# Issuing the first two loads of an attention-score kernel from two engines instead of one

## The chip, the cores and the metric

The kernel runs on one NeuronCore of a Trainium2 chip. The metric is the device time of one execution in microseconds (us): 201.15 us is the median of three executions of the kernel before the change, which took 201.14, 201.15 and 201.38 us. A profiled execution gives the trace on which all other numbers rest; it spans 199.8 us on its own scale, which begins with the first recorded instruction. All times inside an execution are told as microseconds from that start.

## The reference: scaled scores of queries and keys

The inputs are `q` and `k`, both float32 of shape (8, 8, 512, 64): batch, heads, sequence, head dimension. The output is float32 of shape (8, 8, 512, 512).

```python
def reference(q, k):
    scale = 1.0 / np.sqrt(q.shape[-1])
    return (np.einsum('bhqd,bhkd->bhqk', q, k) * scale).astype(np.float32)
```

There are 64 independent products of a 512 x 64 matrix with a 64 x 512 matrix. The inputs are 16.78 MB together and the output is 67.11 MB, so the kernel writes four times what it reads.

## The kernel before: loads, casts, transposes, scores, stores

The batch is cut into four *units* of two batch entries. A unit `v` has one load of `k` and one of `q`, each of 2 MB. They are called k0, q0, k1, q1, k2, q2, k3, q3 here. SyncE issues every one of them, and every transfer goes through SyncE's one hardware DMA queue in that order.

```python
    def xf(v):
        return bigs[(0, 1, 2, 1)[v]]....          # three big buffers, shared with the stores

    def load(v, x):                               # x = 0: k, x = 1: q
        return nc.sync.dma_start(out=xf(v)[:, x], in_=(k_r, q_r)[x][v]...
                                 ).then_inc(load_sems[2 * v + x], 16)

    tc.no_tile_sem_insts.add(load(0, 0).ins.name)   # k0 goes out in the program's opening,
    tc.close()                                      # ahead of the barrier that ends it
    ...
    for n in range(1, 2 * (UNITS - 1)):             # q0, k1, q1, k2, q2 follow the barrier
        load(n // 2, n % 2)
    for x in range(2):                              # k3, q3 reuse the buffer of unit 1:
        nc.sync.wait_ge(sem["ready"], 3 + x)        # wait for the casts of k1 and q1
        load(UNITS - 1, x)
    for g in range(ALL):                            # sixteen stores of 4 MB, in the same queue
        nc.sync.wait_ge(sem["act"], 4 * g + 4)
        nc.sync.wait_ge(sem["dve"], 4 * g + 4)
        nc.sync.dma_start(out=out_r[g], in_=store_buffer(g)...).then_inc(store_sems[g % 3], 16)
```

GpSimd turns each loaded block into bf16, in the order k0, q0, k1, q1 and so on, two instructions for a block. `ready` counts the finished blocks.

```python
    for v in range(UNITS):
        for x in range(2):
            nc.gpsimd.wait_ge(load_sems[2 * v + x], 16)
            ...
            for s in range(2):
                cast = nc.gpsimd.tensor_copy(out=dst, in_=src)     # 128 x 2048, f32 -> bf16
            cast.then_inc(sem["ready"], 1)
```

TensorE transposes the blocks and then computes the scores. The work on the scores is cut into sixteen groups `g` of 4 MB of output; a group has eight pairs of matmuls. ScalarE and VectorE alternate in taking a pair out of PSUM, with the scale multiplied in, into the group's store buffer. Groups 1 and 2 write into buffers that held loads, so they wait until those loads have been cast; from group 3 on, a group waits for an earlier store to land.

```python
    def scores(g, p):
        ...
            if p == 0 and w == 1:
                if g < 3:
                    pe.wait_ge(sem["ready"], (2, 6, 8)[g])
                else:
                    pe.wait_ge(store_sems[g % 3], g // 3 * 16)
            ins = pe.matmul(out=pss[pair % 3][:, w, :], lhsT=qz[:, n, i + w], rhs=keys[:, n], ...)
```

The stores of the groups are called s0 to s15 here. There are three store buffers.

Of the kernel before, what the change touches and what calls it, by code (L numbers as in the profile page):

```python
# [5 lines left out]
def kernel(  # L6
# [5 lines left out]
    nc = tc.nc  # L12
# [3 lines left out]
    UNITS = B // 2  # L16
# [22 lines left out]
    load_sems = [nc.alloc_semaphore(f"load{n}") for n in range(2 * UNITS)]  # L39
# [3 lines left out]
    q_r = q.rearrange("(v b) g (m j) d -> v (b g m) (j d)", b=2, j=R)  # L43
    k_r = k.rearrange("(v b) g (m j) d -> v (b g m) (j d)", b=2, j=R)
# [25 lines left out]
    def xf(v):  # L70
        return bigs[(0, 1, 2, 1)[v]].rearrange("p x i k -> p (x i k)").rearrange(
            "p (x s c) -> p x s c", x=2, s=2)
# [1 line left out]
    def store_buffer(g):  # L74
        return bigs[(0, 2, 1)[g % 3]]

    def load(v, x):
        return nc.sync.dma_start(out=xf(v)[:, x],
                                 in_=(k_r, q_r)[x][v].rearrange("p (s c) -> p s c", s=2)
                                 ).then_inc(load_sems[2 * v + x], 16)  # L80


    tc.no_tile_sem_insts.add(load(0, 0).ins.name)
    tc.close()
    tc.compile()  # L85


    for n in range(1, 2 * (UNITS - 1)):
        load(n // 2, n % 2)
    for x in range(2):  # L90
        nc.sync.wait_ge(sem["ready"], 3 + x)
        load(UNITS - 1, x)
# [62 lines left out]
    for g in range(ALL):  # L155
        c = g + CHUNKS
# [88 lines left out]
```

## Time and profile before

| Quantity | Before |
|---|---|
| median time | 201.15 us |
| span of the profiled execution | 199.8 us |
| TensorE (matmul) busy | 98.2 us, 49% |
| VectorE busy | 106.1 us, 53% |
| ScalarE busy | 84.7 us, 42% |
| GpSimd busy | 39.5 us, 20% |
| DMA traffic | 83.95 MB, mean 420 GB/s |
| loads of k / q, 2 MB each, median from issue to landing | 15.4 / 17.8 us |
| stores, 4 MB each, median from issue to landing | 21.8 us |

A busy share is the part of the span in which an engine had an instruction in execution. The sixteen DMA engines of the core are shared by everything that moves data. A DMA is *issued* by an engine's instruction queue (SPq is that of SyncE), the time until *landing* is that until its last completion signal has arrived, and it includes time spent behind earlier transfers in the same queue.

The chain of waits starts at the last instruction and goes back, at each step, to whatever released it. The timeline lists instructions in order of time, and merges neighbours of one kind: "x14" after a row says that it holds fourteen of them.

### The profile page before, as it was taken

The numbers are of one execution on the slowest core, as the hardware profiler recorded it, in microseconds if no ns is written. First come the engines' busy times: TensorE is split into PE (matmuls) and PEld (weight loads), VectorE is DVE, ScalarE is ACT, GpSimd is POOL, SyncE is SP. The second block draws the span as 40 slices with busy tenths as digits, with TensorE's granted clock in tenths as the row PEclk, the third lists the DMA queues.
The fourth block names the chain that finished last, engine by engine and source line by source line (L and its number), as shares of the span: only waits on it lengthen the run. The fifth ranks groups of instructions, "written<-read, shape, count | busy, mean of one in ns | idle before, by whom it ended". The sixth has DMA issues, their size and how long they took to land.

```text
span 199.8 us, 1074 instructions
## 1 busy us (share of the span) xinstructions
PE 98.2 (49%) x377; PEld 46.7 (23%) x384; DVE 106.1 (53%) x98; ACT 84.7 (42%) x97; POOL 39.5 (20%) x22
## 2 busy tenths in 40 slices
PE   0027660375695637676547646873737373720000
PEld 0026530141442314243124313330202020200000
DVE  4815691074798928476917682767364545440000
ACT  2004670264686726465626653664444343520000
POOL 1299999986000000000000000000000000000000
PEclk9999996578799978889957995799696969685555
DMA  6999999999999999999999999999999999999996
GB/s 207 433 436 426 430 433 433 430 387 430 426 443 426 426 425 431 439 430 423 426 443 433 426 423 436 436 430 423 430 443 430 423 426 436 433 426 430 436 426 275
DMA packets 5509, 83.95 MB, mean 420 GB/s; under 512 B 384, under 2 KB 384, under 8 KB 384
## 3 DMA queue, kind: packets, MB, share of 16 engines
q1 hardware_dynamic: 5504, 83.89, 98.7%
q8 instruction: 3, 0.05, 0.1%
q14 instruction: 2, 0.02, 0.0%
HBM read 16.78 MB, written 67.11 MB: 420 GB/s over the span
## 4 chain that ended last, share of the span: by engine, by line
DMA 53%; DVE 12%; POOL 12%; PE 9%; issue 1%; ACT 1%; SPq 0%
DMA out_dram<-big 42%; POOL xb L122 12%; DVE big L212 10%; DMA big<-in_q_dram 8%; PE ps L145 7%; DMA big<-in_k_dram 4%; PE tp L130 3%; DVE qz L184 2%; DVE kT L184 1%; ACT big L209 1%; SPq L95 0%
## 5 line engine op out<-in xcount | busy, mean ns | idle before, releaser
L145 PE MATMUL ps<-kT,qz 128*128 128x512 bf16 x249 | 78.4, 447 | 63.0 <-DMA out_dram<-big 31.1
L212 DVE TENSOR_SCALAR big<-ps 128x1024 f32<-128x1024 f32 x64 | 77.0, 1223 | 52.0 <-PE ps L145 49.9
L209 ACT ACTIVATE big<-ps 128x1024 f32<-128x1024 f32 x64 | 64.9, 1024 | 71.1 <-PE ps L145 67.9
L145 PEld LDWEIGHTS ps<-kT,qz 128*128 128x128 bf16 x256 | 24.8, 108 | 109.7 <-DMA out_dram<-big 34.5
L122 POOL CAST xb<-big 128x2048 bf16<-128x2048 f32 x16 | 38.8, 2466 | 7.0 <-DMA big<-in_k_dram 6.0
L130 PE MATMUL tp<-identity,xb 128*128 128x128 f32 x104 | 18.9, 343 | 13.6 <-POOL xb L122 13.6
L130 PEld LDWEIGHTS tp<-identity,xb 128*128 128x128 f32 x104 | 17.2, 184 | 17.6 <-issue 16.5
L184 DVE COPY kT<-tp 64x512 f32<-64x512 f32 x14 | 9.7, 694 | 9.0 <-PE tp L130 8.5
L184 ACT COPY kT<-tp 64x512 f32<-64x512 f32 x14 | 8.1, 577 | 14.1 <-PE tp L130 14.0
L184 DVE COPY qz<-tp 64x512 f32<-64x512 f32 x12 | 8.3, 694 | 4.4 <-PE tp L130 4.1
L189 DVE MEMSET qz<- 128x4096 uint32 x2 | 6.9, 3472 | 3.6 <-PEq L85 2.8
L184 ACT COPY qz<-tp 64x512 f32<-64x512 f32 x12 | 7.5, 622 | 2.0 <-PE tp L130 1.8
L130 PE MATMUL ps<-identity,xb 128*128 128x128 f32 x24 | 5.4, 412 | 1.2 <-POOL xb L122 1.2
L130 PEld LDWEIGHTS ps<-identity,xb 128*128 128x128 f32 x24 | 5.0, 226 | 1.6 <-POOL xb L122 1.6
L184 DVE COPY qz<-ps 64x512 f32<-64x512 f32 x4 | 2.8, 695 | 1.9 <-PE ps L130 1.7
L184 ACT COPY qz<-ps 64x512 f32<-64x512 f32 x4 | 2.5, 626 | 2.2 <-PE ps L130 2.2
L184 ACT ACT_TABLE_LOAD x1 | 1.3, 1283 | 1.9 <-PEq L85 1.9
L184 DVE COPY kT<-ps 64x512 f32<-64x512 f32 x2 | 1.4, 694 | 0.3 <-PE ps L130 0.3
L184 ACT COPY kT<-ps 64x512 f32<-64x512 f32 x2 | 1.2, 578 | 0.5 <-PE ps L130 0.5
L102 POOL MEMSET identity<- 128x128 f32 x1 | 0.2, 205 | 1.5 <-POOLq L85 1.5
L104 POOL TENSOR_SCALAR_AFFINE_SELECT identity<-identity 128x128 f32<-128x128 f32 x1 | 0.3, 294 | 0.2 <-POOL identity L102 0.2
L229 POOL MEMSET const-float32-0.0<- 128x1 f32 x1 | 0.1, 100 | 0.2 <-issue 0.2
(3 smaller groups left out, 0.3 us busy)
## 6 DMA issues: line engine op xcount, KB each, us to landing
out_dram<-big SPq DMA_DIRECT2D x16, 4096.0 KB, 21.8
big<-in_k_dram SPq DMA_DIRECT2D x4, 2048.0 KB, 15.4
big<-in_q_dram SPq DMA_DIRECT2D x4, 2048.0 KB, 17.8
```

The costliest lines, as they stand in the source:

```text
L102: nc.gpsimd.memset(identity, 0.0).then_inc(sem["ident"], 1)
L104: nc.gpsimd.affine_select(out=identity, in_=identity, compare_op=mybir.AluOpType.not_equal, fill=1.0, base=0, pattern=[[-1, P]], channel_m ...
L122: cast = nc.gpsimd.tensor_copy(out=dst, in_=src)
L130: ins = pe.transpose(out=dst[:, w], identity=identity, in_=xw[:, c % SLOTS * W + w])
L145: ins = pe.matmul(out=pss[pair % 3][:, w, :], lhsT=qz[:, n, i + w], rhs=keys[:, n], start=True, stop=True)
L184: copy(out=dst, in_=src[:, h]).then_inc(sem["moved"], 1)
L189: engine.memset(qz[:, v * N:(v + 1) * N], 0.0).then_inc(sem["zeroed"], 1)
L209: lambda o, ps: nc.scalar.mul(out=o, in_=ps, mul=scale),
L212: lambda o, ps: nc.vector.tensor_scalar(out=o, in0=ps, scalar1=scale, scalar2=None, op0=mult),
L229: nc = _bacc.Bacc("TRN2", target_bir_lowering=False, num_devices=1)
```

## The change: k0 from SyncE and q0 from ScalarE

The load of q0 is moved from SyncE, where it followed k0 and the opening barrier, to ScalarE, ahead of that barrier. It is for having both blocks of the first unit on their way at once. The other six loads and all stores stay on SyncE, in their order. Nothing is added to or taken from the number of transfers, their sizes or the computation.

```diff
-    def load(v, x):
-        return nc.sync.dma_start(out=xf(v)[:, x],
-                                 in_=(k_r, q_r)[x][v].rearrange("p (s c) -> p s c", s=2)
-                                 ).then_inc(load_sems[2 * v + x], 16)
-
-
-    tc.no_tile_sem_insts.add(load(0, 0).ins.name)
+    def load(v, x, queue=nc.sync):
+        return queue.dma_start(out=xf(v)[:, x],
+                               in_=(k_r, q_r)[x][v].rearrange("p (s c) -> p s c", s=2)
+                               ).then_inc(load_sems[2 * v + x], 16)
+
+
+
+    for x, queue in enumerate((nc.sync, nc.scalar)):
+        tc.no_tile_sem_insts.add(load(0, x, queue).ins.name)
     tc.close()
     tc.compile()
 
 
-    for n in range(1, 2 * (UNITS - 1)):
+    for n in range(2, 2 * (UNITS - 1)):
         load(n // 2, n % 2)
```

## The prediction, made before the changed kernel was run

> **What bounds the kernel now.** I read the rows by slice first, because a kernel with 84 MB of traffic and no engine above 53% is likely to be bound by its transfers.
>
> ```profile
> DMA  6999999999999999999999999999999999999996
> GB/s 207 433 436 426 430 433 433 430 387 430 426 443 426 426 425 431 439 430 423 426 443 433 426 423 436 436 430 423 430 443 430 423 426 436 433 426 430 436 426 275
> ...
> q1 hardware_dynamic: 5504, 83.89, 98.7%
> ```
>
> Each figure stands for one fortieth of the span, 5.0 us. From the second slice to the last but one the DMA engines are busy throughout, at about 430 GB/s, and one queue holds all of it. 83.89 MB at 430 GB/s are 195.1 us; with 1.8 us before the first packet and some 2 us for the slow first packets and the last landings that is the whole span of 199.8 us. So the transfers are the bound, and a change can move the end in two ways only: by making the stream of transfers start earlier or run faster, or by tearing a hole in it.
>
> Next I read the chain of waits in order of time, for its opening, and then the timeline, for how far each issue lies ahead of the transfer it feeds.
>
> ```profile
> 0.74 7.88 DMA big<-in_k_dram
> 8.62 0.06 issue
> 8.68 4.82 POOL xb L122 x2
> 13.49 0.05 issue
> 13.54 4.85 POOL xb L122 x2
> ```
>
> k0 is issued at 0.74 and lands at 8.62; GpSimd begins its casts 0.06 us later. Each block costs it 4.82 to 4.86 us.
>
> ```profile
> 1.92 0.34 SPq L78 DMA_DIRECT2D big<-in_q_dram  x1
> ...
> 8.68 34.21 POOL L122 CAST xb<-big 128x2048 bf16<-128x2048 f32 x14 [6.03 <-DMA big<-in_k_dram]
> 43.62 4.84 POOL L122 CAST xb<-big 128x2048 bf16<-128x2048 f32 x2 [0.74 <-DMA big<-in_q_dram]
> ```
>
> The second row is the important one: fourteen casts, seven blocks, without a gap from 8.68 to 42.89. GpSimd is as fast as the loads, so anything that delays its first cast delays its next six blocks by as much. Only q3, the eighth, has waited for its load, 0.74 us.
>
> ```profile
> 37.99 2.31 PE L145 MATMUL ps<-kT,qz 128*128 128x512 bf16 x5 [7.83 <-POOL xb L122]
> ...
> 48.52 1.96 PE L145 MATMUL ps<-kT,qz 128*128 128x512 bf16 x5 [2.14 <-POOL xb L122]
> ```
>
> These are the starts of groups 1 and 2. Both waited for GpSimd (7.83 and 2.14 us): the buffer they fill has to be cast first, blocks 6 and 8 of the `ready` waits.
>
> ```profile
> 30.95 0.40 SPq L96 DMA_DIRECT2D out_dram<-big  x1
> ...
> 47.15 0.39 SPq L96 DMA_DIRECT2D out_dram<-big  x1
> ...
> 57.32 0.37 SPq L96 DMA_DIRECT2D out_dram<-big  x1
> ...
> 63.93 0.37 SPq L96 DMA_DIRECT2D out_dram<-big  x1
> ...
> DMA to landing us min/median/max: 16.0/21.8/22.6
> ```
>
> Those are the issues of s0 to s3, from the timeline of SyncE. The last row is of all sixteen stores. A store alone takes 9.72 us of the DMA engines: the chain has s3 landing at 82.96 and s6 at 112.11, so (112.11 - 82.96) / 3. A landing after 21.8 us means that such a store was issued a good 12 us before it was needed. The shortest, 16.0 us, is s2 (57.32 to 73.28); s1 comes next with 16.4. The early stores have the least lead.
>
> How much lead, exactly? The packet records of the trace, in order of their starts, have the first packet of s0 at 42.06, that of s1 at 51.78 and that of s2 at 61.63. The lead of the issue over the first packet is 11.1, **4.63** and **4.31** us. Part of that is needed: k0, issued into an idle queue at 0.74, had its first packet at 1.76, so an issue takes 1.0 us to bite. The delay that the queue can swallow is therefore 10.1 us at s0, 3.6 us at s1 and 3.3 us at s2.
>
> **What the Trainium skill says.** "DMA: Bandwidth & Descriptors", section "Issuing engines are not separate DMA queues", says that transfers started by different engines run on the same 16 DMA engines and interleave, and that only issue time is saved. The kernel before has one queue in use for loads and stores, so its trace neither supports nor denies this. The same page, section "Queues, rings and completion order", says that each DMA engine takes packets in turn from the queues that have work for it. Again no run of before shows two such queues. In its section on latency the page gives about 0.6 us to the first byte of a hardware-issued transfer; here it was 1.0 us from the start of the issue (0.39 us of which is the issue itself). I use the measured number.
>
> **The change part by part.**
>
> *Removed:* one issue on SyncE after the barrier, 0.34 us. k1 is then issued at about 1.9 instead of 2.31. This is worth nothing, as k1's packets did not begin before 12.3.
>
> *Added:* one issue on ScalarE in the opening, about 0.4 us, at about 0.74. ScalarE has no work before its copies at 15.61, and SyncE's own issue fits ahead of the same barrier, so I put this at nothing as well.
>
> *Moved:* q0 reaches the DMA engines about 1.2 us sooner, but they were not idle. Its packets no longer stand behind those of k0, they alternate with them. A load is 128 packets of 16 KB, eight for each DMA engine, of 0.61 us. Both loads together still take until 13.5, when q0 landed before (1.92 + 11.6, its least time to landing). k0 ends at the fifteenth or so of sixteen packets instead of the eighth: 13.5 - 0.6 = 12.9 us instead of 8.62. **k0 lands 4.3 us later, q0 no sooner.** The two blocks are cast one after another on GpSimd, k0 first, so having q0 sooner would have helped nothing: before, q0 landed just as the cast of k0 ended, at 13.49.
>
> *What follows:* the casts run from 12.9 on without a gap. They shift by 4.3 us up to block 7, and q3 by 4.3 - 0.74 = 3.5 us. k3 is issued at 23.32 + 4.3 = 27.6 and q3 at 28.23 + 4.3 = 32.5. Their packets are due about 31.8 and 36.7, so both still come in time, by over 3 us. s0 goes out at 35.2, 10.1 - 4.3 = 5.8 us in hand. s1 goes out at 47.15 + 4.3 = 51.4, its first packet is possible at 52.4, and the queue ran dry at 51.8: a **hole of about 0.7 us** (4.3 - 3.6). s2 goes out at 57.32 + 3.5 = 60.8, bites at 61.8, and is due at 61.63 + 0.7 = 62.3: no further hole. s3 at 67.4 has about 3 us in hand. From group 4 on, the waits are for landed stores, and the lead of about 12 us is restored.
>
> *The sum:* 0 for the issues, +0.7 for the hole, -0.3 for two corrections. First, the sixteen DMA engines do not run dry together: s0 finished over a stretch of 1.2 us, and an engine that lags loses less. Second, the opening is slow before: the 128 packets of k0 took 0.71 us in the mean instead of 0.61, 8 x 0.1 = 0.8 us for each engine, and two queues with requests outstanding could cover some of this. 201.15 + 0.7 - 0.3 is 201.55, told as 201.5.
>
> **The rivals.**
>
> *A, the delay is hidden entirely.* If ScalarE's issue comes half a microsecond after SyncE's, k0 gets a packet's start, lands at 12.3, and the shift of 3.7 lies at the edge of the 3.6 that s1 can swallow. If the DMA engines served SyncE's queue first, k0 would land at 8.6 as before and nothing at all would move. For it: the bulk of the work is bound by transfers, and the stream is the same. Time 201.0 to 201.3.
>
> *B, the opening gets faster.* Two queues fill the slow first packets; up to 0.8 us are to be had there. Against it: the sixteen engines are each busy from their first packet on, only slowly[...]. Without a hole it makes 200.4 to 200.8.
>
> *C, GpSimd becomes the bound of the first 60 us.* If k0 lands last (ScalarE issues first), the shift is 4.9 or more, and a queue that has run dry restarts as slowly as it did at 1.76, with first packets of about 1.4 us instead of 0.61. Then s1 leaves a hole of 1.3 + 0.8 us, and 202.5 to 203.2 is the time. For it: the leads are small and every term of the shift is one way. Against it: it needs several terms at their worst.
>
> **Range and chances.** The main path is 201.3 to 202.0, A and B pull below, C above. A range of 200.6 to 202.4 should hold it eight times in ten. Two per cent would be 4 us. For the slow side that needs a hole of 4 us, so a shift near 8, and no load can hold k0 back that far; for the fast side it needs bandwidth above the 430 GB/s at which the queue runs. Within 2% is nearly sure: 0.96; faster 0.01; slower 0.03.
>
> **What would show each step right or wrong.** The DMA queue part of the page must list two hardware queues, the new one with 2 MB. In the chain or the timeline GpSimd's first cast must start at about 12.9; a start at 8.7 means that the queues are not served in turn, and one at 13.5 or later that q0 went ahead. The casts must run on without a gap to about 51.9. The issues of s1 and s2 must move from 47.15 and 57.32 to about 51.4 and 60.8, and the fall in GB/s must be in the slice from 50 to 55 us. If the slices there stay at 430 while the issue has moved, my lag of 1.0 us is too long. The prediction would be wrong altogether if ScalarE's issue held up the opening barrier, or if two queues changed the packet time of 0.61 us.

## The result and the profile after

The changed kernel takes 202.70 us (median of 6 executions, 202.35 to 202.97) against 201.28 us for the kernel before beside it (6 executions, 201.14 to 201.60). The ratio is 1.0069, 95% interval 1.0055 to 1.0082: 1.4 us slower, within 2%, and beyond the upper end of the predicted range, 202.4.

The rows by slice and the queues of the changed kernel, from its page:

```profile
DMA  6999999999999999999999999999999999999996
GB/s 254 424 430 443 427 421 430 404 362 424 424 440 430 424 427 434 424 424 440 430 417 421 437 440 424 417 427 424 430 434 427 421 421 434 434 427 421 427 424 284
...
q1 hardware_dynamic: 5360, 81.79, 96.3%
q10 hardware_dynamic: 144, 2.10, 2.5%
```

The second queue, q10, is there, with the 2.10 MB of q0; q1 is SyncE's. The first slice moved more than before (254 against 207 GB/s): the opening is indeed fuller. But the slice from 40 to 45 us fell from 387 to 362, and later slices show 417 to 424 again and again, where the kernel before has 423 at the least. The DMA row shows no dip, and the slice from 50 to 55 us, where the prediction put the hole, has 424.

The chain of waits in order of time, and the casts in the timeline of GpSimd:

```profile
0.74 12.49 DMA big<-in_k_dram
13.23 0.05 issue
13.28 19.58 POOL xb L124 x9
...
13.28 38.21 POOL L124 CAST xb<-big 128x2048 bf16<-128x2048 f32 x16 [10.64 <-DMA big<-in_k_dram]
```

k0 lands at 13.23 instead of 8.62, q0 at 13.40 and so hardly sooner than before (13.48), and all sixteen casts follow one another to 51.49. From the timeline of SyncE come the issues of s0, s1 and s2:

```profile
35.78 0.40 SPq L98 DMA_DIRECT2D out_dram<-big  x1
...
50.70 0.39 SPq L98 DMA_DIRECT2D out_dram<-big  x1
...
60.49 0.37 SPq L98 DMA_DIRECT2D out_dram<-big  x1
```

They are 4.8, 3.6 and 3.2 us later than before. The first packet of s1 starts at 51.96, so its lead is 1.3 us where it was 4.6; that of s2 is 1.4, where it was 4.3.

Did the DMA engines run dry? By the packet records they were idle for 0.01 us in the mean between 51 and 53 us, as little as in the kernel before. So the 1.2 us by which the span grew (201.0 against 199.8) are not in a hole. The windows from 64 to 184 us show where they are. The first row is of the kernel before, the second of the changed one; the columns are the stretch, its length, the busy time and number of instructions of TensorE, weight loads, VectorE, ScalarE and GpSimd, then TensorE's clock, the DMA share and GB/s:

```profile
64.00:184.00 120.00, 67.67 (x250) 28.67 (x252) 68.87 (x64) 57.78 (x64) 0.00 (x0) 0.84 1.01 431
...
64.00:184.00 120.00, 70.62 (x260) 29.33 (x260) 71.86 (x67) 59.20 (x66) 0.00 (x0) 0.82 1.01 427
```

The DMA engines are busy all the time in both, but move 1% less in a microsecond, long after the changed opening is over. The packet records say the same: the 16 KB packets of the last thirteen stores take 0.616 us in the mean, and took 0.612 before. From the first packet of s0 to the end of the last packet there are 158.45 us, and there were 157.38: +1.07 us. Of these, 0.85 us are packet time (the sum over all packets of the stores, a sixteenth of it for each engine: 157.59 against 156.74); the rest lies between packets or in how far apart the engines end. Another 0.16 is that s0 itself begins at 42.22 instead of 42.06.

### The profile page after: what moved, and what is told of

It reads as the page before. It is cut to its first block, busy times and chain, and to the rows that moved or that the text cites. A ratio compares the mean times of both kernels' runs of the same rounds, so it can differ in the third digit from the quotient of the medians.

```text
span 201.0 us, 1081 instructions
## 1 busy us (share of the span) xinstructions
PE 98.9 (49%) x384; PEld 45.6 (23%) x384; DVE 106.1 (53%) x98; ACT 85.0 (42%) x97; POOL 38.9 (19%) x22
## 4 chain that ended last, share of the span: by engine, by line
DMA 46%; POOL 18%; DVE 13%; PE 9%; issue 2%; ACT 1%; SPq 0%
DMA out_dram<-big 40%; POOL xb L124 18%; DVE big L214 10%; DMA big<-in_k_dram 6%; PE ps L147 6%; PE tp L132 3%; DVE qz L186 2%; DVE kT L186 1%; ACT big L211 1%; SPq L97 0%
## 5 line engine op out<-in xcount | busy, mean ns | idle before, releaser
L147 PE MATMUL ps<-kT,qz 128*128 128x512 bf16 x256 | 80.4, 449 | 58.8 <-DMA out_dram<-big 28.5
L124 POOL CAST xb<-big 128x2048 bf16<-128x2048 f32 x16 | 38.2, 2500 | 10.6 <-DMA big<-in_k_dram 10.6
L132 PE MATMUL tp<-identity,xb 128*128 128x128 f32 x104 | 19.6, 351 | 18.2 <-POOL xb L124 18.2
L132 PEld LDWEIGHTS tp<-identity,xb 128*128 128x128 f32 x104 | 17.9, 190 | 22.5 <-issue 21.5
L132 PE MATMUL ps<-identity,xb 128*128 128x128 f32 x24 | 3.5, 304 | 1.4 <-POOL xb L124 1.4
L132 PEld LDWEIGHTS ps<-identity,xb 128*128 128x128 f32 x24 | 3.3, 162 | 1.6 <-POOL xb L124 1.6
```

Of the source, the lines that this page charges most:

```text
L132: ins = pe.transpose(out=dst[:, w], identity=identity, in_=xw[:, c % SLOTS * W + w])
```

## The experiments

Two theories stood at the start. **Shift**: what counts is that the casts, and with them the issues of the first stores, come late. **Queue**: what counts is the second queue, or the interleaved opening, which could leave the sixteen DMA engines in an order in which all later packets are slower. All times below are medians, with the kernel before run on the same chip.

### The shift alone, the queue alone

The first experiment keeps one queue and has GpSimd wait for both loads of unit 0:

```diff
             nc.gpsimd.wait_ge(load_sems[2 * v + x], 16)
+            if v == 0 and x == 0:
+                nc.gpsimd.wait_ge(load_sems[1], 16)
```

> The kernel before, all loads on SyncE's one queue, but GpSimd waits for both k0 and q0 before it casts k0: its first cast starts at about 13.5 instead of 8.7, and the transfers are issued as before. Theory Shift (the later casts bring the issues of q3 and s0 to s2 close to the moment they are needed, and this costs the time): at least as slow as the changed kernel against before, +1.4 to +2.0 us. Theory Queue (the use of a second hardware queue, or the interleaved start that it brings, leaves the DMA engines in an order in which every later packet is slightly longer): 0 to +0.3 us.

Measured: 202.91 us against 201.27, ratio 1.0079 (1.0066 to 1.0092). First cast at 13.41, issue of s1 at 51.26, lead 0.9 us. No second queue, and the whole loss: the theory Queue isn't needed. Here a small hole does show, in the windows around the start of s1 (the last figure is GB/s):

```profile
51.26 0.39 SPq L96 DMA_DIRECT2D out_dram<-big  x1
...
51.00:51.50 0.50, 0.00 (x0) 0.00 (x0) 0.19 (x1) 0.00 (x0) 0.50 (x1) 1.00 1.15 492
51.50:52.00 0.50, 0.37 (x2) 0.21 (x3) 0.00 (x0) 0.00 (x0) 0.08 (x1) 1.00 0.17 66
52.00:52.50 0.50, 0.50 (x4) 0.20 (x2) 0.01 (x1) 0.44 (x1) 0.00 (x0) 1.00 1.16 492
...
64.00:184.00 120.00, 69.48 (x257) 29.08 (x256) 70.22 (x66) 58.68 (x65) 0.00 (x0) 0.82 1.01 426
```

A window books the whole of a packet where the packet starts, so windows this narrow are rough; the packet records make the idle time 0.32 us in the mean of the engines. The larger part of the 1.6 us is again in the last row, 426 GB/s: the packets of the stores together take 1.3 us longer on each engine than in the kernel before.

The next two keep both queues. One undoes the shift of the changed kernel: VectorE, idle at that time, casts k0 while GpSimd casts q0.

```diff
+            if v == 0 and x == 0:                    # GpSimd leaves k0 out
+                continue
 ...
+            engine.wait_ge(load_sems[0], 16)         # VectorE, after its memsets
+            for s in range(2):
+                ...
+                cast = engine.tensor_copy(out=dst, in_=src)    # k0
+            cast.then_inc(sem["ready"], 1)
```

> The changed kernel with both queues, but VectorE, idle then, casts k0 while GpSimd casts q0: both are cast at about 18.2, as in the kernel before, and all later casts run at their old times. Theory Shift: back to the time before, or up to 0.4 us faster. Theory Queue: as slow as the changed kernel, +1.2 to +1.6 us.

Measured: 201.50 us against 201.27, ratio 1.0013 (1.0005 to 1.0021). The issue of s1 is nearly back, at 48.13 (47.15 in the kernel before), its lead is 3.8 us, and the throughput is back entirely:

```profile
48.13 0.39 SPq L98 DMA_DIRECT2D out_dram<-big  x1
...
64.00:184.00 120.00, 70.73 (x255) 29.65 (x255) 68.88 (x64) 57.87 (x64) 0.00 (x0) 0.81 1.01 431
```

So the second queue has no lasting cost. Third, the queues exchanged (k0 from ScalarE, q0 from SyncE):

```diff
-    for x, queue in enumerate((nc.sync, nc.scalar)):
+    for x, queue in enumerate((nc.scalar, nc.sync)):
```

> The changed kernel with the two queues exchanged: k0 from ScalarE, q0 from SyncE. The shift is the same (k0 lands at about 12.9 to 13.5), the order in which the queues are served is not. Theory Shift: +1.4 us as in the changed kernel. Theory Queue, if it is the order of packets that counts: some other number between 0 and +2 us.

Measured: 202.81 us against 201.27, ratio 1.0079 (1.0067 to 1.0091); k0 lands at 13.33, s1 has a lead of 0.9 us, 426 GB/s. It doesn't matter which of the two engines issues which load.

### Two queues without a shift: a miss and its repair

I meant to have both queues in use from the start, and k0 as early as before, by giving each queue half of k0:

```diff
-    tc.no_tile_sem_insts.add(load(0, 0).ins.name)
+    for part, queue in enumerate((nc.sync, nc.scalar)):
+        rows = slice(part * D, (part + 1) * D)          # partitions 0-63, 64-127
+        ins = queue.dma_start(out=xf(0)[rows, 0], in_=k_r[0]...[rows]).then_inc(load_sems[0], 16)
 ...
```

> k0 alone is split over the two queues in the opening, partitions 0 to 63 from SyncE and 64 to 127 from ScalarE; q0 follows on SyncE as before. k0 should land at 8.3 to 8.7, so the casts do not shift. Theory Queue: slower than before by about 1 us, as both queues start together. Theory Shift: equal to before, or up to 0.4 us faster through the fuller opening.

Measured: 207.75 us against 201.27, ratio 1.0311 (1.0289 to 1.0334). Neither theory said this. The windows of its opening (GB/s last), and the chain:

```profile
5.00:10.00 5.00, 0.00 (x0) 0.00 (x0) 4.20 (x2) 0.00 (x0) 0.00 (x0) 1.00 1.04 210
10.00:15.00 5.00, 0.00 (x0) 0.00 (x0) 1.20 (x1) 0.00 (x0) 0.00 (x0) 1.00 0.93 184
...
0.73 15.89 DMA big<-in_k_dram
```

All DMA engines are busy and move half as much: the packets took about 1.3 us instead of 0.61 until about 15 us, when the last packet of k0 ended. The packet records also show that the two halves did not run together. SyncE's 64 packets came first, between 2.1 and 7.2 us, and from 3 us on they took 1.2 to 1.3 us each; the first of ScalarE's began at 6.7 us, though both issues had started at 0.73. So it is not the sharing of the engines by two queues that made these packets slow. The Trainium skill, "DMA: Bandwidth & Descriptors", section "Rules for kernel authors", advises against transfers to disjoint halves of the partitions, as both use the same 16 engines anyway. The run agrees, in that one half followed the other, and shows a larger harm than an unneeded split: half the rate, already with one half alone. Why was not tested. One thing in it serves the question: after s0 it runs at 431 GB/s in the same window, with a lead of 3.5 us on s1, as the whole stream is late and not only the casts.

The repair splits k0 by columns, each half over all 128 partitions:

```diff
+    for s, queue in enumerate((nc.sync, nc.scalar)):
+        ins = queue.dma_start(out=xf(0)[:, 0, s], in_=k_r[0]...[:, s]).then_inc(load_sems[0], 16)
 ...
```

> k0 is split over the two queues by columns, each half over all 128 partitions, in the opening; q0 follows on SyncE. The slow 1.28 us packets of the split by partitions should be gone and k0 should land at 8.2 to 8.7, with no shift. If the longer packets come from the shift, this is as fast as the kernel before, or up to 0.4 us faster through the fuller opening.

Measured: 201.27 us against 201.21, ratio 1.0002 (0.9994 to 1.0010). k0 lands at 8.70, the lead of s1 is 4.7 us, 431 GB/s. Two queues and no shift cost nothing, and gain nothing.

### How much shift it takes

Extra casts on GpSimd, into a spare tile, ahead of those of k0:

```diff
+                for _ in range(1 if v == 0 and x == 0 and s == 0 else 0):      # 3 in the second
+                    nc.gpsimd.tensor_copy(out=spare[_], in_=src)
```

> The kernel before, one queue, with one extra cast (into a spare tile) on GpSimd ahead of those of k0: a shift of 2.45 us, half of that in the changed kernel. s1 is then issued at about 49.6, 2.2 us ahead of the moment its packets are due, instead of 0.9 to 1.3. Theory Near-dry (it takes a lead of about 1 us or less on a store to bring on the longer packets): 0 to +0.2 us, packets of the later stores at 0.612 us. Theory Proportional (every microsecond of shift costs, however much lead is left): about +0.8 us.

> The same with three extra casts: a shift of 7.35 us, one and a half times that of the changed kernel. s1 is issued at about 54.5 and was due at 51.8, so the queue must run dry for about 3.5 us: this is the hole that the prediction expected, at a size at which it can't be missed. A hole alone: +3.0 to +3.6 us. A hole and longer packets afterwards, 0.617 instead of 0.612 us for some 230 packets for each DMA engine: +4.2 to +4.8 us.

The extra casts took 1.9 us each and not 2.45, so the shifts were 1.6 and 5.4 us, smaller than both texts say. With one: 201.38 us against 201.21, ratio 1.0007 (0.9999 to 1.0015), s1 issued at 47.7, lead 3.9, 430 GB/s. The issue moved by only 0.6 us. With three: 203.56 us, ratio 1.0107 (1.0092 to 1.0123), s1 issued at 51.90, lead 0.9, 426 GB/s, and the DMA engines idle for 0.9 us between 51 and 53. The loss of 2.35 us is mainly that hole and 1.3 us of longer packets. So the longer packets don't grow in step with the shift: the 1.6 us of shift brought 0.1 us of them, and 5.4 us no more than the 4.7 us of the wait for both loads.

### A hole made elsewhere

If it is the queue running dry that matters, and not the late casts, a hole at any other place should do the same. SyncE waits for the landing of s7 before it issues s8:

```diff
         nc.sync.wait_ge(sem["dve"], 4 * g + 4)
+        if g == 8:
+            nc.sync.wait_ge(store_sems[7 % 3], 16 * (7 // 3 + 1))
```

> The kernel before, casts unshifted, but SyncE issues s8 only when s7 has landed: a hole of 1.4 to 2.8 us at about 121, in the middle of the kernel, and no other change. If a queue that runs dry is what brings on the longer packets, they are 0.612 us before the hole and 0.617 us after it, and the time is +2.4 to +3.4 us. If the longer packets come from the shifted work of the first 60 us, they stay at 0.612 us, and the time is +1.8 to +2.6 us.

Measured: 204.50 us against 201.21, ratio 1.0159 (1.0145 to 1.0172), +3.3 us. The lead of s8 is 0.9 us. The windows before, in and after the hole:

```profile
64.00:114.00 50.00, 31.64 (x131) 16.05 (x133) 32.18 (x31) 27.59 (x32) 0.00 (x0) 0.84 1.01 431
...
120.00:121.00 1.00, 0.00 (x0) 0.00 (x0) 0.00 (x0) 0.00 (x0) 0.00 (x0) 1.00 0.16 66
121.00:122.00 1.00, 0.35 (x1) 0.13 (x2) 0.00 (x0) 0.00 (x0) 0.00 (x0) 0.69 0.00 0
...
124.00:184.00 60.00, 33.07 (x104) 11.90 (x104) 30.86 (x28) 25.77 (x27) 0.00 (x0) 0.78 1.00 424
```

431 GB/s ahead of the hole, 424 for all of the 60 us after it; in the kernel before, the last window had 430. By the packet records the engines were idle for 2.4 us, and the packets of s8 to s15 took 0.618 us in the mean instead of 0.612. These 8 x 16 packets make 0.7 us for each engine, and 2.4 + 0.7 us are 3.1 of the 3.3.

### The late casts kept, the lead given back

The last test leaves the changed kernel and its late casts alone and repairs only the lead: s1 and s2 go out in halves, the first when half of the group is done.

```diff
+        if g in (1, 2):
+            for x in range(2):
+                nc.sync.wait_ge(sem["act"], 4 * g + 2 * x + 2)
+                nc.sync.wait_ge(sem["dve"], 4 * g + 2 * x + 2)
+                nc.sync.dma_start(out=out_r[g][:, x], in_=store_buffer(g)[:, x]...
+                                  ).then_inc(store_sems[g % 3], 16)
+            continue
 ...
```

> The changed kernel, with its late casts, but s1 and s2 are each issued in two halves of 2 MB, the first as soon as its four pairs are there. The first half of s1 should go out at 46 to 48, four us and more ahead of 51.9, so that the DMA engines never come near to running dry. Theory Near-dry: the packets of all stores stay at 0.612 us and the time is that of the kernel before, 201.0 to 201.6 us, though all casts are as late as in the changed kernel. If the late casts cost the time by another way: 202.4 to 203.0 us, as in the changed kernel.

> The kernel before with s1 and s2 in the same halves: what the halves do by themselves. The lead of s1 was 4.6 us already, so more of it should do nothing: 201.1 to 201.6 us, packets of 0.612 us.

> The changed kernel once more, as it is, for a second profile of it beside the two others. Time 202.3 to 203.0 us. Lead of s1 0.9 to 1.4 us. The packets of the later stores at about 0.617 us; how soon after s1 they reach this may differ from the first profile, in which it took from 72 to 110 us, where the runs with a lead of 0.9 had it from s1 on.

With the halves the changed kernel took 201.81 us against 201.28, ratio 1.0027 (1.0017 to 1.0038). GpSimd begins at 12.97, as late as ever; the first half of s1 leaves at 48.45 with a lead of 3.7 us:

```profile
12.97 38.17 POOL L132 CAST xb<-big 128x2048 bf16<-128x2048 f32 x16 [10.34 <-DMA big<-in_k_dram]
...
48.45 0.35 SPq L100 DMA_DIRECT2D out_dram<-big  x1
...
64.00:184.00 120.00, 69.08 (x251) 28.85 (x255) 69.75 (x65) 58.23 (x65) 0.00 (x0) 0.82 1.00 430
```

The same halves in the kernel before did nothing: 201.37 us, ratio 1.0002 (0.9994 to 1.0010). The changed kernel itself took 202.43 us once more, ratio 1.0059 (1.0046 to 1.0071), with a lead of 1.0 us and 426 GB/s. In this second profile its packets were long from s1 on; in the first, with a lead of 1.3, they became so by degrees: the share of packets over 0.612 us rose from 17% of s1 to 57% of s7 (5% of s7 in the kernel before).

So the lead decides over the throughput, and the lateness of the casts matters for it only through the lead. But half a microsecond is left. In the profile the last packet ends 0.41 us later than before, and 0.25 of that lies ahead of s0, whose first packet comes at 42.31 instead of 42.06. The windows from 38 to 42 us, the last of q3's transfer, in the kernel before, the changed one, the wait for both loads, and the halves:

```profile
38.00:42.00 4.00, 4.00 (x14) 2.59 (x15) 1.23 (x1) 2.05 (x2) 3.99 (x2) 0.50 1.00 381
...
38.00:42.00 4.00, 0.00 (x0) 0.00 (x0) 0.00 (x0) 0.00 (x0) 4.00 (x3) 0.51 1.03 328
...
38.00:42.00 4.00, 0.00 (x0) 0.00 (x0) 0.00 (x0) 0.00 (x0) 4.00 (x3) 0.50 0.98 393
...
38.00:42.00 4.00, 0.36 (x1) 0.13 (x2) 0.00 (x0) 0.00 (x0) 4.00 (x3) 0.50 1.01 311
```

The five profiles in which k0 and q0 were interleaved have 311 to 352 GB/s here; those with one queue, or with k0 split by columns, have 381 to 397. The packets of q3 take 0.69 to 0.76 us in the mean in the former, 0.64 to 0.67 in the latter. In the changed kernel this takes back the whole gain of the opening: k1's first packet came at 11.94 instead of 12.31, but s0's at 42.22 instead of 42.06. Why the interleaving goes with slower packets 25 us later is open, and so is the rest of the half microsecond.

| profiled run | s1 issued | lead of s1 | GB/s, 64 to 184 us | time over before |
|---|---|---|---|---|
| before | 47.15 | 4.6 | 431 | |
| k0 by columns, two queues | 47.05 | 4.7 | 431 | +0.1 |
| before, stores in halves | 44.4 | 7.3 | 431 | +0.1 |
| one extra cast | 47.7 | 3.9 | 430 | +0.2 |
| changed, k0 on VectorE | 48.13 | 3.8 | 431 | +0.2 |
| changed, stores in halves | 48.45 | 3.7 | 430 | +0.5 |
| changed | 50.70 | 1.3 | 427 | +1.4 |
| changed, again | 51.0 | 1.0 | 426 | +1.2 |
| changed, queues exchanged | 50.96 | 0.9 | 426 | +1.5 |
| wait for both loads | 51.26 | 0.9 | 426 | +1.6 |
| three extra casts | 51.90 | 0.9 | 426 | +2.4 |

The split by partitions, with its whole stream late (lead 3.5, 431 GB/s), and the hole at s8 are left out. No run had a lead of s1 between 1.3 and 3.5 us, so where the limit lies is not known. Later leads are not what sets the runs at 426 and 427 GB/s apart: from s5 on they are 8.5 to 12.1 us in the changed kernel and 8.4 to 11.0 in the one before. No version beat the kernel before.

## Why the prediction was wrong

**The bound, right.** The kernel is a stream of transfers, and all that changed the time was in that stream.

**The load of k0, right.** Told 12.9, was 13.23; the two loads shared the DMA engines packet by packet, as the Trainium skill, "DMA: Bandwidth & Descriptors", section "Queues, rings and completion order", has it: of the first 128 packets 65 came from one queue and 63 from the other. Neither issue cost anything: SyncE's next issue, behind the barrier, came at 1.91 us and before at 1.92. (ScalarE was not without work before its copies, as the prediction has it; it loads a table at 1.92 us for 1.28 us, in both kernels, after the issue.) The exchange of queues showed that it doesn't matter which engine issues which load.

**The casts, right.** First cast 13.28 (12.9), last end 51.49 (51.9), no gap.

**The issues of the stores, nearly right.** s0 at 35.78 (35.2), s1 at 50.70 (51.4), s2 at 60.49 (60.8). Group 1 took a little less time than before: from its first matmul to the issue of s1 8.7 us (42.01 to 50.70) instead of 9.2.

**The hole of 0.7 us as the only cost: the step that failed.** The hole was 0.01 us. s1 was issued 0.7 us earlier than told, s0 began 0.16 us later than before, and an issue took 0.9 us to bite and not 1.0, as the runs that did run dry show. The prediction had named this sign, slices that stay at 430 while the issue has moved, and blamed the lag for it; the lag is the smallest of the three. The term was gone, and yet the kernel lost 1.4 us, where 0.4 was told.

**What stood in its place** was not in the prediction's sum at all. It said that the time could move in two ways, a better stream or a hole, and took the 430 GB/s of the rest for fixed. In fact a store that is issued just before the DMA engines run dry is followed by slower packets nearly to the end of the kernel: 0.616 or 0.617 us for a packet instead of 0.612, in all 0.85 us for each engine in the first profile of the changed kernel and 1.25 in the second. The sentence "from group 4 on ... the lead of about 12 us is restored" was near enough for the lead (7.8 to 12.1 us), and wrong in what it implied, that the loss ends there. The last of its signs, a changed packet time of 0.61 us, did come, but two queues are not what brought it: it came with one queue and late casts, and it stayed away with two queues and the lead given back.

**The corrections of -0.3 us, half right.** The opening did get faster, as rival B had it, by 0.37 us at k1. But the last packets of q3 gave it back. The other correction, for engines that do not run dry together, had no hole to apply to. The sum by the profile is therefore 0.16 (start of s0) + 1.07 (the stores, 0.85 of it longer packets) = 1.2, where the prediction had 0.7 - 0.3. The measured 202.70 lies in the 202.5 to 203.2 of rival C, but by luck: its path, a hole of 1.3 + 0.8 us after a k0 that lands last, did not occur.

**The range** reached 202.4, since a hole was the only loss that it allowed for. The 0.96 for a time within 2% held.

## What to carry to other kernels

When a kernel is bound by transfers, give the block that is needed first the DMA engines alone: a second queue with another block splits the rate, the first block lands with the second, and everything that hangs on it moves. Count the lead of each issue over the first packet it feeds, and keep microseconds of it; here 3.5 us or more were safe and 1.3 us were not. And compare GB/s in a late, steady window, too: an issue that came 3.6 us later at 51 us was paid for up to 184 us at least.

## What the runs showed of the hardware that was not expected

- After an issue with a lead of 0.9 to 1.3 us, or after a hole of 2.4 us, the stores ran at 424 to 427 GB/s instead of 430 to 431 up to 184 us, the end of the windows. That the short lead brings this on is shown by two runs that give the lead back (k0 on VectorE, the halves) and by one that takes it away elsewhere (the hole at s8); by what means the DMA engines keep the slower pace is not. In the kernel before, too, the last two stores crept up, to 0.613 and 0.614 us.
- Transfers to partitions 0 to 63 and 64 to 127, each from a queue of its own, ran at 184 to 210 GB/s, half of what one transfer over all partitions reached. The first had no packet of the second beside it until 6.7 us, and was as slow.
- Where two loads were interleaved at 2 to 13 us, the packets of a later load, q3, were slower at 38 to 42 us, 311 to 352 GB/s instead of 381 to 397, in five profiles of five. That the one brings on the other is not shown by an experiment of its own.
